# Modulation sums as two-part rows, with four tiles for their weights

## The chip, the cores and the metric

The kernel runs on one core of one Trainium2 chip. The core has TensorE (matmuls; PE in the profile, its weight loads PEld), VectorE (DVE), ScalarE (ACT), GpSimd (POOL) and SyncE (SP), which issues DMAs. TensorE writes to PSUM banks, the other engines and the DMAs work on SBUF tiles. The metric is the device time of one execution in microseconds (us); lower is better. Each engine runs its own list of instructions in a fixed order, and semaphores make one engine wait for another. The order within an engine's list is set when the kernel is built: a planner takes the instructions in the order of the source and lets one that it holds to be ready go ahead, unless it is tied to its place.

## The reference

One layer of a decoder trunk on 1024 tokens of 1024 channels. Six modulation vectors are made from one condition vector; shift and scale enter ahead of each sub-layer, the gates behind it.

```python
cond = jax.nn.silu(c)
mod = cond @ w_ada[l] + b_ada[l]
shift1, scale1, gate1, shift2, scale2, gate2 = jnp.split(mod[:, None, :], 6, axis=-1)
u = x * (1.0 + scale1) + shift1
hq, hf, hi, hg, rq, rk, rv, rg, ga, gb = jnp.split(u @ w_in[l], split_at, axis=-1)
ya = _hgrn2(hq, hf, hi, hg, lower_bounds[l]) @ w_pa[l]
yb = _retention(rq, rk, rv, rg, positions) @ w_pb[l]
y = (jax.nn.sigmoid(ga) * ya + jax.nn.sigmoid(gb) * yb) @ w_o[l]
x = _layer_norm(DEEPNORM_ALPHA * x + (1.0 + gate1) * y, ln1_g[l], ln1_b[l])
u = x * (1.0 + scale2) + shift2
h = jnp.square(jax.nn.relu(u @ w_up[l] + b_up[l]))
y = h @ w_down[l] + b_down[l]
x = _layer_norm(DEEPNORM_ALPHA * x + (1.0 + gate2) * y, ln2_g[l], ln2_b[l])
```

The change concerns `gate1`, `shift2`, `scale2` and `gate2`: four sums of 1024 values, each over 1024 weights.

## The kernel before

All large products run in two-part arithmetic: `split` makes of a number a rounded part `hi` on ScalarE (L172) and the remainder `lo` on VectorE (L173), and `mm3` issues three matmuls, hi with hi, hi with lo and lo with hi (L177 to L179), in a number format in which TensorE takes 512 columns in one step. Products of the input and output projections go by a scheme of seven products for eight; `seven` (from L434) does this for groups of 256 output columns. One group is seven products of twelve matmuls, in PSUM banks named psd, psa and psc. Its operands are pieces `raw` of the weights, loaded by SyncE (L315, four buffers), added or subtracted by VectorE (L223) and split. The sums of products are made by VectorE (L443, which must have read a bank before TensorE writes the next product into it) and handed to `use`: for gates a sigmoid on ScalarE (L705), a multiplication on VectorE (L707) and a store by GpSimd (L708). `seven` yields three times a group.

The stretch of the kept groups (`build`, L1781 to L1786) runs 24 of these: four of hg, four of ga, then rq, rg, rk, rg for each of four heads. Beside those that are not rq or rk, it advances the generator `ada_rest`, once at each of the group's three yields and once more at the third, so four steps a group.

`ada_rest` (L1174) makes the modulation sums. There are 16 of them, four sections by four groups of 256 columns, each in four parts `q`. One step loads a weight tile `adw` of 256 rows two parts ahead (L1184, two buffers) and adds its two halves, times the condition, to an accumulator of 128 partitions by 256 columns on VectorE (`ada_step`, L575 and L576; the first of a step is tied to its place on VectorE). The sum over the 128 partitions is then left, and two steps later `ada_end` (L1207) makes it:

- for gate1 and gate2 `ada_row` (L1213): a full-precision matmul with a column of ones as the stationary operand gives one row of 256 (L1216), a bias row is loaded (L1218) and added together with 1 (L1219), and GpSimd stores the row in DRAM, in `g_d` (L1220).
- for scale2 and shift2 `ada_cols` (L578): two matmuls with the accumulator as the stationary operand and the ones as a moving column give two columns (L582), and one VectorE operation adds the bias and writes them to the tile `mod` (L584). `ada_cols` serves the start of the kernel, too, for shift1 and scale1.

`out_proj` (L1381) is the second place. It loads the row of gate1 to all partitions (L1385), prepares the last merge (`first`, with `merge_gate`, L1235 to L1239), and runs eight token blocks, each two halves of 24 matmuls. After the first block `coefs` (L1395) makes of scale2 and shift2, taken from `mod`, the tile `u2AB` (L1398 to L1400), and the rows RA and RB. One block later `out_second` turns the normalized block on TensorE (L1463) and applies `u2AB` on ScalarE (L1468).

In the printed code below the diff's functions stand with the line numbers of the profile.

Of the kernel before, what the change touches and what calls it, by code (L numbers as in the profile page):

```python
# [10 lines left out]
F32 = mybir.dt.float32  # L11
F32R = mybir.dt.float32r
# [3 lines left out]
ALU = mybir.AluOpType  # L16
# [87 lines left out]
def drain(g):  # L104
    for _ in g:
        pass
# [20 lines left out]
class Trunk:  # L127
# [390 lines left out]
    def consts(self):  # L518
        nc, i = self.nc, self.i
        cp = self.cp  # L520
        self.cst = cp.tile([P, N_CONST], F32, name="cst")
        crow = self.st.tile([8, P], F32, name="crow")
        nc.scalar.dma_start(crow, i["c"].rearrange("o (k p) -> (o k) p", p=P))
        nc.sync.dma_start(self.cst, i["k_const"])
        rows = self.st.tile([P, P], F32, name="rows")
        nc.gpsimd.memset(rows, 0.0)
        for r0, ap, n in ((B_ADA, i["b_ada"], 48), (B_LB, i["lb_logits"], 8), (B_G1, i["ln1_g"], 8),
                          (B_B1, i["ln1_b"], 8), (B_UP, i["b_up"], 32)):
            nc.scalar.dma_start(rows[r0:r0 + n, :], ap.rearrange("o (k p) -> (o k) p", p=P))
        self.mask8 = cp.tile([P, N_MASK8], U8, name="mask8")  # L530
        self.ident = self.cst[:, K_ID:K_ID + P]
        small = self.small = cp.tile([P, 72], F32, name="small")
        self.ones = small[:, 0:1]
        nc.vector.memset(self.ones, 1.0)
        self.mhalf = self.small[:, 8:16]
        nc.vector.memset(self.mhalf, -0.5)
        c = self.small[:, 16:24]
        pc = self.ps("c", (P, 8))
        nc.tensor.transpose(pc, crow, self.ident[:8, :8])
        nc.vector.tensor_copy(c, pc)  # L540
        sg = self.small[:, 24:32]
        nc.scalar.activation(sg, c, AF.Sigmoid)
        self.cond = self.small[:, 32:40]
        nc.vector.tensor_tensor(self.cond, c, sg, op=ALU.mult)

        self.mod = cp.tile([P, 48], F32, name="mod")
        self.cols = cp.tile([P, P], F32, name="cols")
        self.rows = rows

# [624 lines left out]
    def ada_rest(self):  # L1174

        ap = self.aw
        parts = [(s, g, q) for s, g in ADA_ORDER for q in range(4)]
        loaded = {}

        def load(n):  # L1180
            s, g, q = parts[n]
            c0 = s * D + 256 * g
            t = loaded[n] = ap.tile([P, 2, 256], F32, tag="adw", bufs=2, name=self.uid("adw"))
            self.nc.sync.dma_start(t, self.i["w_ada"][256 * q:256 * q + 256, c0:c0 + 256].rearrange("(k p) c -> p k c", p=P))  # L1184

        load(0)
        load(1)
        yield
        ends = None
        for n, (s, g, q) in enumerate(parts):  # L1190
            if q == 0:
                acc = ap.tile([P, 256], F32, tag="adacc", bufs=2, name=self.uid("acc"))
            w = loaded.pop(n)
            for j in (0, 1):
                r = self.ada_step(acc, w[:, j], 2 * q + j, q + j == 0)
                if j == 0:
                    self.tc.keep_in_program_order(r)
            if n + 2 < len(parts):
                load(n + 2)
            if q == 1 and ends is not None:  # L1200
                ends()
            if q == 3:
                ends = lambda acc=acc, s=s, g=g: self.ada_end(acc, s, g)
            yield
        ends()

    def ada_end(self, acc, sec, g):  # L1207
        if sec in (S_SHIFT2, S_SCALE2):
            self.ada_cols(acc, sec, 2 * g, 2, 1.0 if sec == S_SCALE2 else 0.0, self.ps("b", (P, 2)))
        else:  # L1210
            self.ada_row(acc, sec, g)

    def ada_row(self, acc, sec, g):  # L1213
        nc = self.nc
        pr = self.ps("b", (1, 256))
        nc.tensor.matmul(pr, self.ones, acc, start=True, stop=True)  # L1216
        br = self.aw.tile([1, 256], F32, tag="brow", bufs=1, name=self.uid("brow"))
        nc.sync.dma_start(br, self.i["b_ada"][0:1, sec * D + 256 * g:sec * D + 256 * g + 256])  # L1218
        nc.vector.scalar_tensor_tensor(br, pr, 1.0, br, op0=ALU.add, op1=ALU.add)  # L1219
        nc.gpsimd.dma_start(self.g_d[sec][0:1, 256 * g:256 * g + 256], br)  # L1220


# [158 lines left out]
    def out_proj(self, first):  # L1381
        nc, V, i = self.nc, self.nc.vector, self.i
        op = self.op
        s2, h2 = self.mod[:, S_SCALE2 * 8:S_SCALE2 * 8 + 8], self.mod[:, S_SHIFT2 * 8:S_SHIFT2 * 8 + 8]
        g1 = self.row(op, self.g_d[S_GATE1], "g1")  # L1385
        xts = []

        def x_rows(t):
            xts.append(self.wr.tile([P, D], F32, tag="raw", bufs=4, name=self.uid("xt")))
            nc.sync.dma_start(xts[t], i["x"][t * P:(t + 1) * P, :])  # L1390

        x_rows(0)
        x_rows(1)

        def coefs():  # L1395
            AB = op.tile([P, 16], F32, name="u2AB")
            A, B = AB[:, 0:8], AB[:, 8:16]
            V.tensor_tensor(A, self.cols[:, B_G1:B_G1 + 8], s2, op=ALU.mult)  # L1398
            V.tensor_tensor(B, self.cols[:, B_B1:B_B1 + 8], s2, op=ALU.mult)
            V.tensor_tensor(B, B, h2, op=ALU.add)  # L1400
            RA = self.row(op, i["ln1_g"], "RA")
            RB = self.row(op, i["ln1_b"], "RB")
            V.tensor_scalar(RA, RA, ALPHA, None, op0=ALU.mult)
            for j in range(2):
                js = slice(j * 512, j * 512 + 512)
                tt = op.tile([P, D], F32, tag="zp", bufs=1, name=self.uid("rb"))
                t0, t1 = tt[:, :512], tt[:, 512:]
                nc.sync.dma_start(t0, self.g_d[S_GATE2][:, js].to_broadcast([P, 512]))
                nc.sync.dma_start(t1, i["b_down"][:, js].to_broadcast([P, 512]))
                V.tensor_tensor(t0, t0, t1, op=ALU.mult)  # L1410
                V.scalar_tensor_tensor(RB[:, js], RB[:, js], ALPHA, t0, op0=ALU.mult, op1=ALU.add)
            return A, B, RA, RB

        def y_parts(t):
            yh = self.wp.tile([P, 8, P], F32R, tag="wh", bufs=3, name=self.uid("yh"))
            yl = self.wp.tile([P, 8, P], F32R, tag="wl", bufs=3, name=self.uid("yl"))
            for q in (0, 1):
                ks = slice(4 * q, 4 * q + 4)
                self.split(yh[:, ks], yl[:, ks], self.y[q, t // 4][:, :, t % 4 * P:t % 4 * P + P])
            return yh, yl  # L1420

        ys = [y_parts(0)]
        first()
        ys.append(y_parts(1))
        for t in range(8):
            yh, yl = ys.pop(0)
            if t < 6:
                ys.append(y_parts(t + 2))
            xt = xts[t]
            z = op.tile([P, D], F32, tag="z", bufs=2, name=self.uid("z"))  # L1430
            stat = op.tile([P, 32], F32, tag="stat", bufs=2, name=self.uid("stat"))
            for ch in (0, 1):
                cs = slice(ch * 512, ch * 512 + 512)
                po = self.ps("d" if t else "c")
                for k in range(KT):
                    self.mm3(po, yh[:, k], yl[:, k], self.wo[k][0][:, 0, cs], self.wo[k][1][:, 0, cs], k == 0, k == KT - 1)
                V.tensor_tensor(z[:, cs], po, g1[:, cs], op=ALU.mult)
                V.scalar_tensor_tensor(z[:, cs], xt[:, cs], ALPHA, z[:, cs], op0=ALU.mult, op1=ALU.add)
                V.bn_stats(stat[:, 6 * ch:6 * ch + 6], z[:, cs])
            mv, rs = self.norm_stats(stat)  # L1440
            nm = stat[:, 24:25]
            V.scalar_tensor_tensor(nm, mv[:, 0:1], -1.0, rs, op0=ALU.mult, op1=ALU.mult)
            nc.scalar.activation(z, z, AF.Identity, scale=rs, bias=nm)
            if t < 6:
                x_rows(t + 2)
            self.tick()
            if t == 0:
                cf = coefs()
            self.later(1, lambda t=t, z=z: self.out_second(t, z, *cf))
            if t == 6:  # L1450
                self._split_to(self.w_next + 1)
# [220 lines left out]
def build(ctx, tc, ins, out):  # L1672
# [15 lines left out]
             for j in range(FT // 2)]  # L1688
    k.b12_d = k.dp.tile([P, 2048], F32, name="b12_d")
    k.z2_d = [k.dp.tile([P, D], F32, name=f"z2_d{t}") for t in range(8)]  # L1690
    k.g_d = {s: k.dp.tile([1, D], F32, name=f"g_d{s}") for s in (S_GATE1, S_GATE2)}
    w_in = ins["w_in"]


# [207 lines left out]
```

## Time and profile before

| | |
|---|---|
| median of 3 runs | 2258.92 us (2257.53 to 2260.2) |
| profiled execution | 2258.29 us |
| its span, first to last instruction | 2256.5 us |
| granted TensorE clock over the span | 0.997 |
| stretch of the kept groups and the modulation sums | 312 to 797 us |
| output projection, first blocks | 1533 to 1557 us |

A row of the timeline reads: start in us from the start of the span, duration, engine, line, operation, out<-in by the program's tiles with buffer numbers left out, shapes, count; in brackets the idle time just before it and what ended it. A row of the waits reads: who waited, for whom, microseconds in total, times, the longest. A row of the groups reads: line, engine, operation, tiles, shapes, count, busy microseconds, mean nanoseconds of one, and idle time ahead of them. A matmul's record is longer than the distance to the next one's start, since matmuls overlap. "psb" is the bank that the modulation sums use.

### The profile page before, as it was taken

To read this page: it belongs to the slowest core of one execution; us is meant where nothing else is said; L and a number is where in the kernel's file an instruction comes from. 1 tells how busy PE (TensorE), PEld (TensorE's weight loads), DVE (VectorE), ACT (ScalarE), POOL (GpSimd) and SP (SyncE) were. 2 spreads that over 40 slices of the span, in tenths; PEclk is the share of its full clock that TensorE was granted. 3 is DMA by queue.
4 is the path that set the end of the run, shared out by engine and by line. 5 is a ranking of instruction groups with operands and counts; after the bars stand their busy time and mean duration, and the time that the engine had idled before them with its cause. 6 is when DMAs were issued, how large, how long until landed. Compare 5 with 4: busy or idle time off the path is not lost. (4 is left out here: it accounts for less than half of the span.)

```text
span 2256.5 us, 29106 instructions
## 1 busy us (share of the span) xinstructions
PE 2215.7 (98%) x10214; PEld 1822.1 (81%) x10214; DVE 1660.4 (74%) x3024; ACT 967.3 (43%) x1625; POOL 282.1 (13%) x444
## 2 busy tenths in 40 slices
PE   6999999999999999999999999999999999999997
PEld 4888887888888888888877777888878888888886
DVE  7757777667878678889765556977796665577669
ACT  3533334433333333332354434443575555553441
POOL 0110111111111101010112221112112112100001
PEclk9999999999999999999999999999999999999999
DMA  9554644544343522113176667655344444787653
GB/s 309 183 167 161 208 136 164 169 135 140 135 141 117 172 89 75 57 66 104 60 254 201 209 204 258 211 163 179 112 150 156 152 154 151 265 289 247 215 164 131
DMA packets 229075, 375.33 MB, mean 166 GB/s; under 512 B 17096, under 2 KB 127424, under 8 KB 228672
## 3 DMA queue, kind: packets, MB, share of 16 engines
q1 hardware_dynamic: 200176, 279.66, 38.4%
q0 software_dynamic: 28432, 93.35, 11.2%
q8 instruction: 80, 1.31, 0.2%
q14 instruction: 67, 0.55, 0.1%
q10 hardware_dynamic: 320, 0.45, 0.1%
HBM read 275.87 MB, written 97.53 MB: 165 GB/s over the span
## 5 line engine op out<-in xcount | busy, mean ns | idle before, releaser
L177 PE MATMUL psd<-U,bh 128*128 128x512 f32 x616 | 241.9, 393 | 1.8 <-DVE e L443 1.8
L178 PE MATMUL psd<-U,bh 128*128 128x512 f32 x616 | 239.8, 389 | 0.0
L179 PE MATMUL psd<-U,bl 128*128 128x512 f32 x616 | 239.8, 389 | 0.0
L172 ACT ACTIVATE bh<-s 128x512 fp32r<-128x512 f32 x204 | 128.6, 631 | 239.7 <-PE psd L178 78.9
L178 PE MATMUL psd<-U,wh 128*128 128x512 f32 x504 | 199.6, 396 | 3.6 <-DVE U L173 3.3
L177 PE MATMUL psd<-U,wh 128*128 128x512 f32 x504 | 202.4, 405 | 0.4 <-ACT U L172 0.4
L179 PE MATMUL psd<-U,wl 128*128 128x512 f32 x504 | 201.8, 400 | 0.0
L172 ACT ACTIVATE bh<-raw 128x512 fp32r<-128x512 f32 x153 | 97.1, 638 | 206.1 <-PE psd L178 100.4
L173 DVE TENSOR_TENSOR bl<-raw,bh 128x512 fp32r<-128x512 f32 x153 | 104.5, 689 | 105.8 <-ACT bh L172 92.9
L173 DVE TENSOR_TENSOR bl<-s,bh 128x512 fp32r<-128x512 f32 x204 | 139.5, 685 | 49.4 <-ACT bh L172 49.3
L177 PEld LDWEIGHTS psd<-U,bh 128*128 128x128 f32 x616 | 115.6, 188 | 31.0 <-issue 3.5
L172 ACT ACTIVATE U<-hr 128x512 fp32r<-128x512 f32 x112 | 70.5, 630 | 151.0 <-issue 56.7
L179 PEld LDWEIGHTS psd<-U,bl 128*128 128x128 f32 x616 | 115.7, 188 | 24.2
L178 PEld LDWEIGHTS psd<-U,bh 128*128 128x128 f32 x616 | 115.7, 188 | 23.5
L172 ACT ACTIVATE wh<-raw 128x512 fp32r<-128x512 f32 (+1 forms) x78 | 52.7, 695 | 173.8 <-PE psd L178 136.2
L177 PE MATMUL psa<-U,bh 128*128 128x512 f32 x312 | 121.4, 389 | 0.0
L178 PE MATMUL psa<-U,bh 128*128 128x512 f32 x312 | 121.4, 389 | 0.0
L179 PE MATMUL psa<-U,bl 128*128 128x512 f32 x312 | 121.4, 389 | 0.0
L178 PEld LDWEIGHTS psd<-U,wh 128*128 128x128 f32 x504 | 95.5, 190 | 25.3 <-DVE U L173 7.3
L177 PEld LDWEIGHTS psd<-U,wh 128*128 128x128 f32 x504 | 95.1, 190 | 19.1 <-ACT U L172 2.3
L179 PEld LDWEIGHTS psd<-U,wl 128*128 128x128 f32 x504 | 95.3, 189 | 18.7
L173 DVE TENSOR_TENSOR U<-hr,U 128x512 fp32r<-128x512 f32 x112 | 76.7, 685 | 44.7 <-ACT U L172 44.5
(446 smaller groups left out, 5630.7 us busy)
## 6 DMA issues: line engine op xcount, KB each, us to landing
raw<-in_w_in SPq DMA_DIRECT2D x126, 512.0 KB
raw<-in_w_down SPq DMA_DIRECT2D x48, 512.0 KB
raw<-in_w_pb SPq DMA_DIRECT2D x36, 512.0 KB
adw<-in_w_ada SPq DMA_DIRECT2D x64, 256.0 KB
raw<-in_w_up SPq DMA_DIRECT2D x32, 512.0 KB
adw<-in_w_ada SPq DMA_DIRECT2D x16, 512.0 KB
rv_d<-e POOLq DMA_DIRECT2D x32, 256.0 KB, 3.8
rg_d<-e POOLq DMA_DIRECT2D x32, 256.0 KB, 2.4
```

The source lines that it names most:

```text
L172: pin(self.nc.scalar.activation(hi, src, AF.Copy))
L173: pin(self.nc.vector.tensor_tensor(lo, src, hi.bitcast(F32), op=ALU.subtract))
L177: r = mm(out, wh, uh, start=start, stop=False, skip_group_check=more)
L178: mm(out, wh, ul, start=False, stop=False, skip_group_check=more)
L179: return r, mm(out, wl, uh, start=False, stop=stop, skip_group_check=more)
```

## The change

- All four sections become rows. `ada_end` is gone, and `ada_rest` no longer calls `ada_cols`. `mod` shrinks to the 16 columns of shift1 and scale1.
- A row is made in two parts: the accumulator is split into `hi` (ScalarE) and `lo` (VectorE, tied to its place), and two matmuls with a column of ones add both up in one bank. The number format is that of the large products.
- `ada_row` is a generator: bias load and `hi` in one step, `lo` in the next, the matmuls in the next, the bias addition (tied to its place) and the store in the last. With each part of the next sum it advances by one.
- The weight tiles `adw` have four buffers instead of two, the bias row two instead of one; loads are issued two parts ahead, as before.
- At the output projection two small DMAs bring the rows of scale2 and shift2 as 8 x 128 each into a tile of 16 partitions, and `coefs` turns it on TensorE into 16 columns in PSUM, from which `u2AB` is made.
- The scratch for the descriptors of GpSimd's DMAs is set to 4096 bytes a partition; before, nothing was set.

```diff
-        self.mod = cp.tile([P, 48], F32, name="mod")
+        self.mod = cp.tile([P, 16], F32, name="mod")
...
-            t = loaded[n] = ap.tile([P, 2, 256], F32, tag="adw", bufs=2, name=self.uid("adw"))
+            t = loaded[n] = ap.tile([P, 2, 256], F32, tag="adw", bufs=4, name=self.uid("adw"))
...
+        ones = ap.tile([P, 1], F32R, name="ones_r")
+        self.nc.scalar.activation(ones, self.ones, AF.Copy)
         load(0)
         load(1)
         yield
-        ends = None
+
+        ends = iter(())
...
             if n + 2 < len(parts):
                 load(n + 2)
-            if q == 1 and ends is not None:
-                ends()
+            next(ends, None)
             if q == 3:
-                ends = lambda acc=acc, s=s, g=g: self.ada_end(acc, s, g)
+                ends = self.ada_row(acc, s, g, ones)
             yield
-        ends()
-
-    def ada_end(self, acc, sec, g):
-        if sec in (S_SHIFT2, S_SCALE2):
-            self.ada_cols(acc, sec, 2 * g, 2, 1.0 if sec == S_SCALE2 else 0.0, self.ps("b", (P, 2)))
-        else:
-            self.ada_row(acc, sec, g)
-
-    def ada_row(self, acc, sec, g):
-        nc = self.nc
+        drain(ends)
+
+    def ada_row(self, acc, sec, g, ones):
+
+        nc, ap = self.nc, self.aw
+        pin = self.tc.keep_in_program_order
+        hi, lo = (ap.tile([P, 256], F32R, tag="ad" + e, bufs=1, name=self.uid("ad" + e)) for e in "hl")
+        br = ap.tile([1, 256], F32, tag="brow", bufs=2, name=self.uid("brow"))
+        nc.sync.dma_start(br, self.i["b_ada"][0:1, sec * D + 256 * g:sec * D + 256 * g + 256])
+        nc.scalar.activation(hi, acc, AF.Copy)
+        yield
+        pin(nc.vector.tensor_tensor(lo, acc, hi.bitcast(F32), op=ALU.subtract))
+        yield
         pr = self.ps("b", (1, 256))
-        nc.tensor.matmul(pr, self.ones, acc, start=True, stop=True)
-        br = self.aw.tile([1, 256], F32, tag="brow", bufs=1, name=self.uid("brow"))
-        nc.sync.dma_start(br, self.i["b_ada"][0:1, sec * D + 256 * g:sec * D + 256 * g + 256])
-        nc.vector.scalar_tensor_tensor(br, pr, 1.0, br, op0=ALU.add, op1=ALU.add)
+        nc.tensor.matmul(pr, ones, hi, start=True, stop=False)
+        nc.tensor.matmul(pr, ones, lo, start=False, stop=True)
+        yield
+        plus = 0.0 if sec == S_SHIFT2 else 1.0
+        pin(nc.vector.scalar_tensor_tensor(br, pr, plus, br, op0=ALU.add, op1=ALU.add))
         nc.gpsimd.dma_start(self.g_d[sec][0:1, 256 * g:256 * g + 256], br)
...
     def out_proj(self, first):
...
-        s2, h2 = self.mod[:, S_SCALE2 * 8:S_SCALE2 * 8 + 8], self.mod[:, S_SHIFT2 * 8:S_SHIFT2 * 8 + 8]
         g1 = self.row(op, self.g_d[S_GATE1], "g1")
+        mrow = op.tile([16, P], F32, name="mrow")
+        for j, sec in enumerate((S_SCALE2, S_SHIFT2)):
+            nc.sync.dma_start(mrow[8 * j:8 * j + 8], self.g_d[sec].rearrange("o (k p) -> (o k) p", p=P))
...
         def coefs():
             AB = op.tile([P, 16], F32, name="u2AB")
+            m2 = self.ps("a", (P, 16))
+            nc.tensor.transpose(m2, mrow, self.ident[:16, :16])
+            s2, h2 = m2[:, 0:8], m2[:, 8:16]
...
-    k.g_d = {s: k.dp.tile([1, D], F32, name=f"g_d{s}") for s in (S_GATE1, S_GATE2)}
+    k.g_d = {s: k.dp.tile([1, D], F32, name=f"g_d{s}") for s in (S_GATE1, S_SHIFT2, S_SCALE2, S_GATE2)}
...
-    nc = bacc.Bacc("TRN2", target_bir_lowering=False, num_devices=1)
+    nc = bacc.Bacc("TRN2", target_bir_lowering=False, num_devices=1, dynamic_dma_scratch_size=4096)
```

## The prediction

> **What bounds the kernel.** I read the page's busy shares first, then a table of busy time by stretch, then TensorE's waits in the longest stretch that the change touches, and then the timeline around each of its instructions.
>
> ```profile
> PE 2215.7 (98%) x10214; PEld 1822.1 (81%) x10214; DVE 1660.4 (74%) x3024; ACT 967.3 (43%) x1625; POOL 282.1 (13%) x444
> ...
> 312.00:797.00 485.00, 483.19 (x2133) 394.41 (x2132) 359.85 (x625) 186.21 (x316) 60.20 (x112) 1.00 0.45 148
> ...
> PE psd L177 <- DVE e L443: 1.8, 3, 0.7
> ```
>
> TensorE is busy for 98% of the span. The second row gives a stretch, its length, each engine's busy time (TensorE, its weight loads, VectorE, ScalarE, GpSimd), the granted clock and the DMA share. In the stretch from 312 to 797 us, in which the modulation sums are made beside the kept gates, it is busy for 483.19 of 485 us at a granted clock of 1.00. The last row is all that it waited for there: three waits, 1.8 us together. So whatever only unburdens VectorE, ScalarE or a queue can bring these 1.8 us and the restarts behind them, and no more. Otherwise the span moves by what TensorE itself is given to do, and the main term of the sum is what a modulation sum costs on TensorE.
>
> **Removed from TensorE.** Its busy time doesn't show that cost, because matmuls overlap; the distance from start to start does.
>
> ```profile
> 350.61 0.39 PE L177 MATMUL psd<-U,bh 128*128 128x512 f32 x1
> ...
> 353.11 0.39 PE L179 MATMUL psd<-U,bl 128*128 128x512 f32 x1
> 353.42 0.59 PE L1216 MATMUL psb<-acc,small 128*1 128x256 f32 x2
> 353.95 0.50 PE L177 MATMUL psd<-U,bh 128*128 128x512 f32 x1
> 354.29 0.40 PE L178 MATMUL psd<-U,bh 128*128 128x512 f32 x1
> ...
> 550.48 0.39 PE L179 MATMUL psd<-U,bl 128*128 128x512 f32 x1
> 550.71 0.50 PE L582 MATMUL psb<-small,acc 128*128 128x1 f32 x4
> 551.07 0.49 PE L177 MATMUL psd<-U,bh 128*128 128x512 f32 x1
> 551.39 0.40 PE L178 MATMUL psd<-U,bh 128*128 128x512 f32 x1
> ...
> L1219 DVE SCALAR_TENSOR_TENSOR brow<-psb,brow 1x256 f32<-1x256 f32 x8 | 3.2, 405 | 0.0
> ...
> L584 DVE SCALAR_TENSOR_TENSOR mod<-psb,cols 128x2 f32<-128x2 f32 x8 | 1.3, 158 | 1.4 <-PE psb L582 1.3
> ```
>
> From 350.61 to 353.11 lie eleven steps between matmuls of 512 columns, so one step is 0.227 us. Around the row sum, two such steps (353.11 to 354.29) take 1.18 instead of 0.454 us: a full-precision row costs 0.73 us. Around the column sum they take 0.91 (550.48 to 551.39): it costs 0.46 us. The last two rows count them, eight of each: 8 x 0.73 + 8 x 0.46 = **9.5 us removed**.
>
> **Added to TensorE: sixteen rows in two parts.** Each is two matmuls of 256 columns with one stationary column, in the number format of the large matmuls around them. No row shows that form. From below, a 512-column step halved is 0.114, so a row costs 0.23; from above, it costs the 0.73 of the full-precision row. I take 0.30: the format is that of the matmuls before and after, which follow each other without a gap, and 0.07 is left for what a change of shape may cost. So 16 x 0.30 = **4.8 us added** (3.6 to 11.7).
>
> [...]
>
> **What the parts cost the other engines.** Each row needs a copy `hi` on ScalarE and a subtraction `lo` on VectorE, both 128x256.
>
> ```profile
> L173 DVE TENSOR_TENSOR bl<-raw,bh 128x512 fp32r<-128x512 f32 x70 | 47.6, 689 | 38.8 <-ACT bh L172 26.2 <-PE psb L1216 12.4
> ...
> L173 DVE TENSOR_TENSOR U<-U,U 128x1024 fp32r<-128x1024 f32 x2 | 2.4, 1224 | 1.1 <-ACT U L172 1.1
> ...
> L172 ACT ACTIVATE bh<-raw 128x512 fp32r<-128x512 f32 x70 | 45.2, 646 | 112.5 <-PE psd L178 64.1 <-issue 27.1 <-DVE e L727 14.3
> ```
>
> 512 elements more cost VectorE 535 ns, so 256 elements take about 689 - 268 = 421 ns (estimate); half of ScalarE's 646 and some fixed part give about 0.4. Sixteen subtractions are 6.7 us. Eight additions of 405 ns replace eight of 158: 2.0 more. VectorE goes from 359.85 to some 369 of 485 us, ScalarE from 186 to 193. Both have free time in the stretch, so by themselves these cost nothing; without that cover they would be 8.7 us. Eight more bias loads on SyncE and eight more row stores on GpSimd are hidden by those queues' waiting.
>
> **Four tiles for the weights.** Loads are still issued two parts ahead, but into a buffer whose last reader finished long ago.
>
> ```profile
> SPq L1184 <- DVE acc L576: 345.7, 61, 18.3
> ...
> 498.40 0.37 SPq L1184 DMA_DIRECT2D adw<-in_w_ada  x1
> 499.04 1.08 SPq L315 DMA_DIRECT2D raw<-in_w_in  x2
> ...
> 504.97 0.69 DVE L223 TENSOR_TENSOR s<-raw,raw 128x512 f32<-128x512 f32 x1 [3.58 <-DMA raw<-in_w_in]
> ...
> 508.24 0.69 DVE L443 TENSOR_TENSOR e<-psd,e 128x512 f32<-128x512 f32 x1
> ...
> 508.99 0.50 PE L177 MATMUL psd<-U,bh 128*128 128x512 f32 x1 [0.67 <-DVE e L443]
> 509.32 0.40 PE L178 MATMUL psd<-U,bh 128*128 128x512 f32 x1
> ```
>
> SyncE's 345.7 us of waiting for the accumulation should go, but TensorE felt them only in the three waits. The one at 508.99 shows the way: a 256 KB weight load starts 0.64 us ahead of two 512 KB projection pieces; they land at 504.97, VectorE starts its burst late, and L443 frees the bank late. One MB in 5.9 us is 0.17 MB per us, so the load ahead takes about 1.5 us. Issued earlier, it is out of the way. Against this, the bias addition now sits in that part, before the split that frees the pieces: 0.4 later. A wait also costs a slow restart (0.33 for a step of 0.227). All three waits gone would be 1.8 + 3 x 0.1 = 2.1 us. I take **-1.3** (-2.1 to +1.3, three waits longer by the 0.4).
>
> **At the output projection.** Two small DMAs, one transpose and three VectorE operations that now wait for it.
>
> ```profile
> 1538.83 0.38 SPq L1369 DMA_DIRECT2D g<-g_d  x1
> 1539.32 0.37 SPq L1235 DMA_DIRECT2D gbr<-gb_d  x1
> ...
> 1541.20 0.15 DVE L1398 TENSOR_TENSOR u2AB<-cols,mod 128x8 f32<-128x8 f32 x1
> ...
> 1541.47 1.30 DVE L1400 TENSOR_TENSOR u2AB<-u2AB,mod 128x8 f32<-128x8 f32 x1
> ...
> 1544.39 0.69 DVE L1238 TENSOR_TENSOR U<-psb,gbr 128x512 f32<-128x512 f32 x1 [1.62 <-DMA gbr<-gb_d]
> ...
> 1556.26 1.09 PE L1463 MATMUL psa<-cst,z 128*128 128x128 f32 x8 [0.94 <-ACT z L1443]
> ```
>
> The DMAs go behind g on SyncE's queue and push the merge's gate load (1539.32) back by about 0.7 us. VectorE waits for that load until 1544.39, and the chain from there to the z of the first token block is what TensorE waits for at 1556.26. The three coefficient operations lay in VectorE's idle time from 1541.20 on; behind the transpose, which in the source follows the first block's 48 matmuls, they fall into the same chain: 3 x 0.15. So that wait grows by about **1.1 us** (0, if the order leaves both out of the chain, to 2.3, if one of the three takes 1.30 as the last did). The transpose waits for the small DMAs, and the second block's matmuls stand behind it; the first block's 10.9 us (48 x 0.227) should cover their landing. The transpose itself is **0.25** (from 0.14, an eighth of the 1.09 above, to 0.73).
>
> **At the stretch's end** the last row, now in more steps, holds its buffers longer.
>
> ```profile
> L1220 POOL DMA_DIRECT2D g_d<-brow x8: 505/505/523, 356.6 to 514.9; - x8
> ...
> DMA to landing us min/median/max: 1.9/2.8/3.3
> ...
> 791.43 3.44 SPq L315 DMA_DIRECT2D raw<-in_w_in  x4
> ...
> 800.00:804.00 4.00, 4.00 (x19) 3.34 (x18) 0.00 (x0) 1.20 (x2) 0.00 (x0) 1.00 1.04 365
> ...
> 804.02 0.63 ACT L172 ACTIVATE wh<-raw 128x512 fp32r<-128x512 f32 x1 [2.82 <-PE psd L178]
> ```
>
> Copy, subtraction, matmuls, addition (0.4 each, 0.3 for the matmuls), the issue (0.5) and the landing (2.8) of a store are 4.8 us. SyncE's queue, with four weight loads, may wait for that release; its transfers, done by 804 now (DMA share 1.04 up to there), would then be done by 809. The split at 804.02 could come that much later. It prepares a weight tile two ahead of the one in use, so TensorE need not notice, and I take nothing (up to 4.8, if VectorE's work behind that split is late for TensorE).
>
> **The sum.** -9.5 + 4.8 - 1.3 + 1.1 + 0.25 = -4.65 us. The profiled execution took 2258.29 (span 2256.5 and 1.8 around it), so it would take 2253.6; from the median shown, 2258.92, **2254.3 us**.
>
> **Rivals.**
>
> (1) *TensorE waits for `lo`.* Before, the accumulated tile was long done when its matmul came up. Now the matmul needs a VectorE result of the same step.
>
> ```profile
> 354.62 0.68 DVE L707 TENSOR_TENSOR e<-e,psd 128x512 f32<-128x512 f32 x1
> ...
> 355.95 1.50 DVE L576 SCALAR_TENSOR_TENSOR acc<-adw,small,acc 128x256 f32<-128x256 f32 x3
> ...
> DVE s L223 <- DMA raw<-in_w_in: 44.3, 22, 3.6
> ```
>
> The subtraction would come behind the first of the three at 355.95 and end near 356.85, 3.4 us after the place of today's row. The order on TensorE is fixed when the kernel is built; if it puts the row too early, every matmul behind it waits. The three waits above show that such an order can err by 0.6 us when VectorE is late, and VectorE waited 22 times for pieces. With 0.3 us for each of 16 rows the gain is gone: -4.65 + 4.8, or 2259.1 (chance 0.19). With 0.6 it is -4.65 + 9.6: **2263.9, slower**; slower by over 0.2% from 0.57 us a row on (chance 0.13). For it: nothing separates `lo` and its matmul in the source's steps. Against it: in 21 of 24 groups TensorE met no late VectorE.
>
> (2) *The two-part row is as dear as the full-precision one*: 16 x 0.73 = 11.7, so -4.65 + 6.9: 2261.2 (0.06).
>
> (3) *All falls well*: rows of 0.23, no waits, nothing at the output projection: -9.5 + 3.6 - 2.1 + 0.15 = -7.85: 2251.1 (0.10).
>
> (4) *GpSimd's stores wait for room in a smaller descriptor scratch.*
>
> ```profile
> q0 software_dynamic: 28432, 93.35, 11.2%
> ...
> or_d<-ot POOLq DMA_DIRECT2D x32, 256.0 KB, 4.8
> ```
>
> 28432 packets are 1777 on each of 16 engines. The slowest frequent store lands after 4.8 us; if one store ahead of the norm's power on GpSimd had to wait so long, the end moves by up to 4.8: 2259.1 (0.03). [...]
>
> (5) *The four tiles do nothing*, since loads are still two ahead: without the -1.3, 2255.6. It lies within the forecast's own range, 2251.8 to 2256.8 (0.46). Some other shift of the built order: 0.03.
>
> **Range and chances.** A measurement of this kernel can tell about 0.2%, 4.5 us, from no change: below 2254.4 is faster, above 2263.4 slower. The forecast sits on the first bound, and I give 0.32 of its 0.46 to faster, since its large terms are measured and only 0.30 a row is chosen. With (3), 0.10, and 0.03 of the rest: faster 0.45. Same: 0.14 + 0.18 + 0.06 + 0.02 = 0.40. Slower: 0.13 + 0.02 = 0.15. The range reaches from 2249 to 2263.5: below it is only the lower end of (3), above it most of the slower case, together some 0.15.
>
> **What would show it.** Right: 16 rows at which two steps take about 0.75 us in place of 1.18 and 0.91; no wait of TensorE in the stretch; SyncE's wait for the accumulation near zero; TensorE's wait at the first block's transposes near 2 us. Wrong: a TensorE wait named after `lo` at the rows (rival 1), a row's two steps near 1.2 (rival 2), or a transpose of the sums that waits for its small DMAs.

## The result, and the profile after

The changed kernel takes 2268.36 us (median of 6 runs, 2266.34 to 2274.94), the kernel before 2258.31 us (6 runs, 2256.36 to 2260.2). The ratio is 1.0054 [1.0044, 1.0064]: **0.5% slower**, 14 us above the forecast and 5 us above its range. The profiled execution took 2268.21 us, 9.9 more than the one of before.

The first fence has rows of the page of the changed kernel, the second its busy time by stretch (columns as in the prediction), the third the later of these stretches in the kernel before, the fourth the changed kernel's waits of TensorE and VectorE from 312 to 807 us.

```profile
PE 2217.7 (98%) x10199; PEld 1822.4 (80%) x10199; DVE 1664.3 (73%) x3040; ACT 973.8 (43%) x1642; POOL 287.5 (13%) x452
...
L177 PE MATMUL psd<-U,bh 128*128 128x512 f32 x616 | 242.4, 393 | 11.3 <-DVE e L443 11.3
```

```profile
312.00:480.00 168.00, 168.00 (x747) 137.69 (x747) 118.77 (x214) 74.11 (x128) 20.70 (x39) 1.00 0.52 167
480.00:797.00 317.00, 305.72 (x1331) 247.91 (x1330) 242.08 (x421) 113.40 (x197) 41.40 (x77) 0.99 0.41 132
```

```profile
480.00:797.00 317.00, 315.19 (x1400) 259.52 (x1400) 246.22 (x422) 114.28 (x194) 37.09 (x69) 1.00 0.42 140
```

```profile
PE psd L177 <- DVE e L443: 11.3, 7, 2.2
...
DVE s L223 <- DMA raw<-in_w_in: 54.4, 22, 5.1
```

TensorE's busy share is still 98%, and up to 480 us it waits for nothing. The loss is in the second part of the stretch: 305.72 us busy of 317, where the kernel before is busy for 315.19. The 1.8 us of waits for L443 have become 11.3, in seven waits in place of three, and VectorE's wait for the projection pieces has grown from 44.3 to 54.4 us.

Where the time went is seen when the same instruction is found in two traces. The table gives by how many us a ScalarE instruction starts later (+) or earlier (-) than in the profiled execution of the kernel before. Each kernel is described below.

| at (us) | changed | e2 | e6 | e7 | e11 |
|---|---|---|---|---|---|
| 310, stretch begins | -2.1 | -1.6 | -1.0 | -1.3 | -1.2 |
| 500 | -5.1 | -4.4 | -1.0 | -1.3 | -4.2 |
| 800, stretch over | +7.1 | -6.5 | +8.2 | -0.8 | -5.0 |
| last one | +9.9 | -7.2 | +7.8 | -0.6 | -4.8 |

The first line differs by a microsecond or two between executions whatever the kernel. From 310 to 500 the changed kernel gains 3.0 us; from 500 to 800 it loses 12.2. The stretch as a whole costs 9.2 of the 9.9; what follows scatters by a few us each way.

One of the seven stalls, of the changed kernel, by engine in the timeline (GpSimd, SyncE, VectorE, TensorE):

```profile
614.12 0.54 POOL L708 DMA_DIRECT2D rg_d<-e  x1 [2.26 <-DVE e L707]
614.83 0.51 POOL L1226 DMA_DIRECT2D g_d<-brow  x1 [0.17 <-issue]
```

```profile
614.25 0.37 SPq L1184 DMA_DIRECT2D adw<-in_w_ada  x1
615.20 1.30 SPq L315 DMA_DIRECT2D raw<-in_w_in  x2
```

```profile
614.14 0.41 DVE L1225 SCALAR_TENSOR_TENSOR brow<-psb,brow 1x256 f32<-1x256 f32 x1
614.47 1.27 DVE L173 TENSOR_TENSOR bl<-raw,bh 128x512 fp32r<-128x512 f32 x2
...
621.96 0.69 DVE L223 TENSOR_TENSOR s<-raw,raw 128x512 f32<-128x512 f32 x1 [5.13 <-DMA raw<-in_w_in]
...
625.24 0.68 DVE L443 TENSOR_TENSOR e<-psd,e 128x512 f32<-128x512 f32 x1
```

```profile
623.38 0.39 PE L179 MATMUL psc<-U,bl 128*128 128x512 f32 x1
625.98 0.80 PE L177 MATMUL psd<-U,bh 128*128 128x512 f32 x1 [2.21 <-DVE e L443]
626.57 0.63 PE L178 MATMUL psd<-U,bh 128*128 128x512 f32 x1
627.00 0.63 PE L179 MATMUL psd<-U,bl 128*128 128x512 f32 x1
...
630.12 0.40 PE L179 MATMUL psd<-U,bl 128*128 128x512 f32 x1
630.36 0.28 PE L1221 MATMUL psb<-adh,ones_r 128*1 128x256 f32 x1
630.48 0.39 PE L177 MATMUL psd<-U,bh 128*128 128x512 f32 x1
```

The row's end (bias addition L1225, store L1226) now falls right ahead of two 512 KB pieces of the next projection weight. The store stands on GpSimd's queue behind the 256 KB store of the kept gate (`rg_d`), 0.37 us before the pieces are issued. VectorE uses them at 621.96, 6.8 us after their issue; in the kernel before it was 4.7 in the groups without a stall and 5.9 in the three with one. VectorE's burst starts late, L443, which stands behind that first L223 in VectorE's fixed order, frees the bank late, and TensorE waits 2.2 us. In the kernel before the row's end came two steps earlier, in part 1 of the next sum and not in part 3; no pair of pieces follows there.

The last three lines show a new row: 630.12 to 630.48 is 0.36 for a step of 0.227, so its first matmul costs 0.13. All sixteen rows, taken so, cost 4.2 us.

### The profile page after: what moved, and what is told of

The parts are those of the page before. It is cut to its first block, busy times and chain, and to the rows that moved or that the text cites. A ratio compares the mean times of both kernels' runs of the same rounds, so it can differ in the third digit from the quotient of the medians.

```text
span 2266.4 us, 29143 instructions
## 1 busy us (share of the span) xinstructions
PE 2217.7 (98%) x10199; PEld 1822.4 (80%) x10199; DVE 1664.3 (73%) x3040; ACT 973.8 (43%) x1642; POOL 287.5 (13%) x452
## 3 DMA queue, kind: packets, MB, share of 16 engines
q0 software_dynamic: 28688, 93.36, 11.1%
## 5 line engine op out<-in xcount | busy, mean ns | idle before, releaser
L177 PE MATMUL psd<-U,bh 128*128 128x512 f32 x616 | 242.4, 393 | 11.3 <-DVE e L443 11.3
```

The lines of the kernel that those rows point to most:

```text
L177: r = mm(out, wh, uh, start=start, stop=False, skip_group_check=more)
```

## The experiments

Three theories at first. **A**: the row's store delays the pieces behind it. **B**: the bias addition, ahead of the pieces' splits on VectorE, delays their issue and use. **C**: the four tiles change the order of the loads. Behind e8 two more share A between them: **S**, the store's packets of 64 bytes are what hurts, and **Q**, any store at that place in GpSimd's queue. The ratio is to the kernel before, run beside each group of experiments; its medians there were 2257.62 to 2258.87 us, so a difference between runs of different groups is good to about 1 us. "Waits" are TensorE's for L443 from 312 to 807 us.

| | us (range, runs) | ratio to before | waits: us, times, longest |
|---|---|---|---|
| e1 | 2259.92 (2258.21 to 2262.79, 10) | 1.0008 [0.9999, 1.0018] | 6.5, 7, 1.3 |
| e2 | 2252.84 (2251.0 to 2257.11, 10) | 0.998 [0.9971, 0.999] | 1.5, 2, 0.8 |
| e3 | 2270.13 (2266.37 to 2272.36, 4) | 1.0056 [1.0041, 1.0071] | 14.2, 7, 3.1 |
| e4 | 2256.45 (2253.78 to 2261.02, 10) | 0.9996 [0.9987, 1.0006] | 3.0, 3, 1.2 |
| e5 | 2267.32 (2265.11 to 2270.63, 4) | 1.0044 [1.0027, 1.0061] | 11.1, 7, 2.1 |
| e6 | 2269.24 (2266.03 to 2271.89, 4) | 1.0047 [1.0032, 1.0062] | 10.2, 6, 2.0 |
| e7 | 2257.33 (2255.87 to 2260.17, 10) | 0.9998 [0.9989, 1.0007] | 2.1, 3, 1.0 |
| e8 | 2259.3 (2255.69 to 2259.8, 10) | 1.0002 [0.9992, 1.0011] | 3.4, 3, 1.2 |
| e9 | 2268.23 (2266.68 to 2271.1, 4) | 1.0044 [1.0027, 1.0061] | 11.4, 6, 2.2 |
| e10 | 2257.44 (2256.21 to 2260.68, 10) | 1.0002 [0.9992, 1.0011] | 3.2, 3, 1.3 |
| e11 | 2254.12 (2251.39 to 2258.14, 10) | 0.9978 [0.9969, 0.9987] | 1.8, 4, 0.6 |
| e12 | 2253.64 (2251.38 to 2259.41, 10) | 0.9981 [0.9971, 0.999] | 1.1, 1, 1.1 |

**e1, the store one step later.** In the changed kernel, with room for two rows on their way and three bias rows:

```diff
         pin(nc.vector.scalar_tensor_tensor(br, pr, plus, br, op0=ALU.add, op1=ALU.add))
-        nc.gpsimd.dma_start(self.g_d[sec][0:1, 256 * g:256 * g + 256], br)
+        yield
+        pin(nc.gpsimd.dma_start(self.g_d[sec][0:1, 256 * g:256 * g + 256], br))
```

> The changed kernel with one thing moved: the row's store to DRAM is issued one step later (behind the second gate store of its group instead of the first), while the bias addition stays where it is on VectorE; a third bias buffer carries the row over. Theory A (the store's sixteen 64-byte packets, sent 0.37 us ahead of two 512 KB weight pieces, delay these by about 1.2 us, and TensorE waits): pieces land 4.7 to 5.9 us after issue instead of 5.9 to 7.1, TensorE's waits for L443 in the stretch fall from 11.3 to about 3 us, the stretches of half clock behind waits of 2.2 us vanish, 2257 us. Theory B (VectorE's bias addition ahead of the pieces' splits, and TensorE arriving earlier, make the waits): nothing changes, 2268 us. Theory C (the order of the four weight tiles' loads): nothing changes, 2268 us.

8.4 us come back, so the store's place is most of the loss. Seven waits stay, shorter. In them the pieces are used 5.0 to 6.2 us after their issue.

**e2, bias addition and store two steps later**, and so in part 1 again, of the sum after the next:

```diff
         nc.tensor.matmul(pr, ones, lo, start=False, stop=True)
         yield
+        yield
+        yield
         plus = 0.0 if sec == S_SHIFT2 else 1.0
```

> The changed kernel with bias addition and store both moved two steps later, to the group's third yield, where the row's end stood before. Theories A and B: the waits go back to those of before or fewer, 2254 to 2256 us (the two-part rows' saving of about 5.3 us is then left). B alone against A: the gain over the run with only the store moved is then 3 us or more; with A alone it is 1 to 2 us, the 0.3 us by which the pieces are issued sooner. Theory C: 2266 to 2268 us.

15.5 us faster than the changed kernel, and apart from the same room for more rows as in e1 the only edit is the place of the row's end. It is 0.2% faster than the kernel before. Five of its seven uses of a pair come 4.6 to 4.75 us after the issue. In the other two (6.0 and 6.1) the packets show a 16 KB instruction fetch beside the pieces; these two are its waits.

**e3, two weight tiles** in the changed kernel, and **e4, four tiles and the smaller descriptor scratch** in the kernel before:

```diff
-            t = loaded[n] = ap.tile([P, 2, 256], F32, tag="adw", bufs=4, name=self.uid("adw"))
+            t = loaded[n] = ap.tile([P, 2, 256], F32, tag="adw", bufs=2, name=self.uid("adw"))
```

```diff
-            t = loaded[n] = ap.tile([P, 2, 256], F32, tag="adw", bufs=2, name=self.uid("adw"))
+            t = loaded[n] = ap.tile([P, 2, 256], F32, tag="adw", bufs=4, name=self.uid("adw"))
...
-    nc = bacc.Bacc("TRN2", target_bir_lowering=False, num_devices=1)
+    nc = bacc.Bacc("TRN2", target_bir_lowering=False, num_devices=1, dynamic_dma_scratch_size=4096)
```

> The changed kernel with two weight tiles instead of four. Theory A and theory B: as the changed kernel, 2266 to 2270 us, waits of 10 to 12 us. Theory C (four tiles put a weight load 0.96 instead of 0.64 us ahead of the pieces and another between them): 2258 to 2261 us, waits of 2 to 4 us.

> The kernel before with four weight tiles and the smaller descriptor scratch alone, no rows changed. Theory A and theory B: as before, 2257 to 2260 us, TensorE's waits in the stretch 1 to 3 us. Theory C: 2265 us or more. If the smaller scratch slows GpSimd's stores, it shows here as well, as stores that land later than 2.4 us.

C falls: with two tiles the changed kernel is as slow, and four tiles and the small scratch cost the kernel before nothing. The -1.3 us of the forecast lies within the interval of e4, and so does nothing at all.

**e5, the store alone put back.** e2, with room for one row and one bias row more, and in it

```diff
         pin(nc.vector.scalar_tensor_tensor(br, pr, plus, br, op0=ALU.add, op1=ALU.add))
-        nc.gpsimd.dma_start(self.g_d[sec][0:1, 256 * g:256 * g + 256], br)
+        yield
+        yield
+        pin(nc.gpsimd.dma_start(self.g_d[sec][0:1, 256 * g:256 * g + 256], br))
```

**e6 and e7, more stores in the kernel before**: sixteen at the bad place (e6) and fifteen, of the sum before, at the good one (e7; `prev` is that sum's accumulator). They go to a scratch `g_x` in DRAM that is declared for them, and nobody reads what they store:

```diff
             if q == 3:
+                self.tc.keep_in_program_order(self.nc.gpsimd.dma_start(self.g_x[0:1, 64 * (n - q):64 * (n - q) + 256], acc[0:1, :]))
                 ends = lambda acc=acc, s=s, g=g: self.ada_end(acc, s, g)
```

```diff
             if q == 1 and ends is not None:
                 ends()
+                self.tc.keep_in_program_order(self.nc.gpsimd.dma_start(self.g_x[0:1, 64 * (n - q):64 * (n - q) + 256], prev[0:1, :]))
```

**e8, a VectorE operation more in the kernel before:**

```diff
             if q == 3:
+                self.tc.keep_in_program_order(self.nc.vector.scalar_tensor_tensor(acc, acc, 1.0, acc, op0=ALU.mult, op1=ALU.max))
                 ends = lambda acc=acc, s=s, g=g: self.ada_end(acc, s, g)
```

> The kernel of e2 (2252.84 us) with only the store of the row moved two further steps on, so that it stands again where a pair of 512 KB pieces is about to be issued; the bias addition stays at its late, harmless place, and VectorE's and TensorE's orders are those of e2. Theory A (the store's 64-byte packets delay the pieces): its 8.4 us come back, 2261, with TensorE's waits for L443 near 7 us. Theory B (the bias addition in front of the splits is what counts, the store only goes with it): 2253, waits near 1.5 us. If the cost of the store needs both, something between.

> The kernel before, whose row ends stay where they are, with one more store of 1 KB in each of the sixteen groups, of the first row of the accumulated tile to a scratch in DRAM, on GpSimd right after the group's last accumulation, where the changed kernel has its row's store. VectorE, TensorE and ScalarE run their old order. Theory A: some 8 us slower than before, 2266, with TensorE waiting for L443 in most of the later groups. Theory B: as before, 2258.

> The same sixteen extra stores in the kernel before, two steps later, beside the row ends of the kernel before, where no pair of pieces follows. Theory A and theory B: as before, 2258 (to 2260), so that a slower e6 is due to the place and not to sixteen more transfers. If it is as slow as e6, the place doesn't matter.

> The kernel before with one more VectorE operation in each group at that place, right after the group's last accumulation and ahead of the pieces' splits: the accumulated tile times 1.0, maximum with itself (128x256, some 0.45 us, leaves the values as they are). No store is added. Theory B: the pieces' buffers come free and their splits end later, TensorE waits for L443: 5 to 7 us slower, 2263 to 2265. Theory A: VectorE has free time, 2258 to 2260.

These settle A. The store alone, put back into e2, costs 14.5 us (2267.32 - 2252.84); e6 loses 10.9 us to before and e7 nothing, by the same store at another place, and in both the other engines keep the order of the kernel before (in e6 but for one instruction of VectorE and one of SyncE, near 800 us). Six of seven pairs in e6 meet the store 0.23 us ahead of them and stall; at the seventh it is issued 2.65 us behind the first piece (and the kept gate's store 2.12 us behind it), the pieces are used after 4.3 us, and TensorE doesn't wait. A large store ahead of the small one in the queue doesn't do the harm by itself: in six of e7's later groups the small store stands 0.53 us behind a gate's store, too, and there the next piece, a single one, follows 1.87 us behind it. e8 shows no loss, but tells less of B than meant: in the later groups its operation came between the splits that free the two pieces, so that only the second was issued later, by 0.33 us.

The pair of e6 that is looked at next, with the queues of GpSimd and SyncE and the first use:

```profile
538.49 0.51 POOL L1203 DMA_DIRECT2D g_x<-acc  x1
```

```profile
538.73 1.08 SPq L315 DMA_DIRECT2D raw<-in_w_in  x2
```

```profile
545.86 0.69 DVE L223 TENSOR_TENSOR s<-raw,raw 128x512 f32<-128x512 f32 x1 [4.78 <-DMA raw<-in_w_in]
```

What the store does to the transfers is seen in a table by stretch: one pair of pieces in e7 and the same pair in e6, in 1 us from 1 us behind the first piece's issue. The last two columns are the DMA engines' mean busy share and GB/s.

```profile
538.29:539.29 1.00, 1.00 (x6) 0.84 (x5) 0.34 (x1) 1.00 (x2) 0.00 (x0) 1.00 0.88 300
539.29:540.29 1.00, 1.00 (x6) 0.81 (x5) 0.35 (x1) 0.11 (x1) 0.00 (x0) 1.00 1.03 378
540.29:541.29 1.00, 1.00 (x6) 0.84 (x5) 0.00 (x0) 0.28 (x1) 0.00 (x0) 1.00 1.10 380
541.29:542.29 1.00, 1.00 (x6) 0.84 (x5) 0.22 (x1) 0.35 (x1) 0.00 (x0) 1.00 1.02 359
542.29:543.29 1.00, 1.00 (x6) 0.81 (x6) 1.00 (x3) 0.00 (x0) 0.00 (x0) 1.00 0.27 91
```

```profile
539.72:540.72 1.00, 1.00 (x6) 0.84 (x5) 0.33 (x1) 1.00 (x2) 0.00 (x0) 1.00 0.92 315
540.72:541.72 1.00, 1.00 (x6) 0.82 (x5) 0.36 (x1) 0.12 (x1) 0.00 (x0) 1.00 0.76 239
541.72:542.72 1.00, 1.00 (x6) 0.83 (x5) 0.00 (x0) 0.28 (x1) 0.00 (x0) 1.00 0.86 201
542.72:543.72 1.00, 1.00 (x6) 0.84 (x5) 0.00 (x0) 0.36 (x1) 0.00 (x0) 1.00 0.80 250
543.72:544.72 1.00, 1.00 (x6) 0.81 (x6) 0.00 (x0) 0.00 (x0) 0.00 (x0) 1.00 0.91 315
544.72:545.72 1.00, 1.00 (x6) 0.84 (x5) 0.00 (x0) 0.00 (x0) 0.00 (x0) 1.00 0.35 121
545.72:546.72 1.00, 1.00 (x7) 0.81 (x5) 0.86 (x2) 0.00 (x0) 0.00 (x0) 1.00 0.19 66
```

Without the store all sixteen engines are busy and move 360 to 380 GB/s until the pieces are there. With it the transfers run at 200 to 250 GB/s in the same microseconds, with engines idle although a megabyte is due, and end in a tail in which a few engines catch up. The drop begins with the store: its sixteen packets start from 2.0 to 2.9 us behind the first piece's issue, which is the second row of e6. A store of 1 KB costs the pieces some 2.4 us (used after 7.14 in e6, 4.78 in e7).

**e9 and e10, which property of the store.** e6 with sixteen rows of 1 KB, and e6 with the store on SyncE's queue:

```diff
+                self.tc.keep_in_program_order(self.nc.gpsimd.dma_start(self.g_x[4 * (n - q):4 * (n - q) + 16, :], acc[0:16, :]))
```

```diff
+                self.tc.keep_in_program_order(self.nc.sync.dma_start(self.g_x[0:1, 64 * (n - q):64 * (n - q) + 256], acc[0:1, :]))
```

> e6 again (the kernel before with a store on GpSimd at the bad place, 2269.24 us), but of sixteen rows of 1 KB in place of one: sixteen packets of 1024 bytes, where e6 has sixteen of 64. Theory S (the size: packets of 64 bytes hold up the engines that carry the pieces): 2258 to 2260, though 16 KB move instead of 1. Theory Q (any store at this place, queued on GpSimd behind the 256 KB store of the kept gate, has the pieces wait): 2266 to 2270.

> e6 again, with its 1 KB store issued by SyncE, between the two pieces, in place of GpSimd, and so not behind the 256 KB store of the kept gate. The second piece is issued some 0.4 us later for it. Theory S: as slow as e6, 2266 to 2270, if SyncE's store is cut into packets of 64 bytes too. Theory Q: 2258 to 2261.

S falls: sixteen packets of 1024 bytes are as bad as sixteen of 64 (2268.23 and 2269.24 us). Q fits both runs, but the queue isn't shown alone. From SyncE, where the packets show the row as one of 1024 bytes, the store costs nothing, though it stands between the two pieces and puts the second off to 0.97 us or more behind the first. So e10 changes three things at once: the queue, one packet in place of sixteen, and the place behind the first piece. No run separates them. These are the two queues of e10 around the same pair:

```profile
538.35 0.54 POOL L708 DMA_DIRECT2D rg_d<-e  x1 [2.32 <-DVE e L707]
```

```profile
538.48 0.37 SPq L1184 DMA_DIRECT2D adw<-in_w_ada  x1
539.11 0.37 SPq L315 DMA_DIRECT2D raw<-in_w_in  x1
539.53 0.50 SPq L1203 DMA_DIRECT2D g_x<-acc  x1
540.08 0.37 SPq L315 DMA_DIRECT2D raw<-in_w_in  x1
```

**e11 and e12, the store from SyncE** in the changed kernel and in e2:

```diff
-        nc.gpsimd.dma_start(self.g_d[sec][0:1, 256 * g:256 * g + 256], br)
+        nc.sync.dma_start(self.g_d[sec][0:1, 256 * g:256 * g + 256], br)
```

> The changed kernel with one word altered: the row's store is issued by SyncE in place of GpSimd, at the same step, and so not behind the kept gate's 256 KB store. The bias addition stays at its early place. VectorE's built order moves the first two L223 of the later groups behind one more operation, since the pieces now stand behind the store. Theory Q with a bias addition that costs nothing by itself: 2252 to 2254, as e2. Theory Q with the bias addition's early place worth the 7 us that lie between e1 and e2: 2258 to 2261. If GpSimd's queue is not the point: 2268.

> e2 (bias addition and store both at the late place, 2252.84 us) with the store issued by SyncE. VectorE's and TensorE's orders are those of e2. Theory Q: at the late place GpSimd's store did no harm, so 2252 to 2254, the same; if its packets still cost something there, 2250 to 2251.

One word turns the changed kernel into one of 2254.12 us, 14.2 us faster and 0.2% faster than the kernel before. But the built order of VectorE changes with it, so that this isn't the worth of the store's queue alone. e12, whose VectorE order is that of e2, adds nothing to e2. The three fast versions (e2, e11, e12) can't be told apart.

B is left half open. In e11 the bias addition keeps its early place, and the pieces are still used late (5.3 to 6.4 us after their issue), yet TensorE's waits are 1.8 us: in each of the seven groups the order built for VectorE has an L443 and a split ahead of the first L223 that stand behind it in the changed kernel, so that late pieces hold up less. In e1, with VectorE in the order of the changed kernel, the pieces come as late (5.0 to 6.2), and the early bias addition goes with 6.5 us of waits and 7.1 us more than e2. So an early bias addition can cost, next to a tight order; on top of the harmful store it added at most 1.0 us (2268.36 against e5, whose ranges overlap).

## Why the prediction was wrong

**The rows: right.** Removed 9.5, added 4.8 foretold; added 4.2 measured, 0.26 a row (0.24 where both matmuls stand together). The forecast's lower bound, half of a 512-column step for each of a row's two matmuls, was 0.23 a row: the trace is within 0.03 of it. With 9.5 less 4.2, 5.3 us, this term is about the gain that e2, e11 and e12 show (4.8 to 5.4 us).

**The row stores: the step that failed.** "Eight more bias loads on SyncE and eight more row stores on GpSimd are hidden by those queues' waiting." The step counted the new stores and not the new place of all sixteen: behind the kept gate's store and just ahead of two pieces. GpSimd is busy for only 62.1 of the 485 us from 312 to 797 (20.70 and 41.40); what isn't hidden is the transfer, which meets the loads that set TensorE's pace. Foretold 0, measured 14.5 (e5 against e2). The trace of the changed kernel accounts for it: 11.3 - 1.8 = 9.5 of waits, 0.16 for each of four more waits (a matmul is drawn 0.39 long and followed after 0.227), and 3.7 more for restarts (5 of 0.15 and 2 of 1.7, against 3 of 0.15): 13.8. Less the 5.3 saved at the rows, that is 8.5; the stretch lost 9.2.

**Four tiles, -1.3: wrong in its reason, small in its size.** "Issued earlier, it is out of the way" did not come true. SyncE's waits ahead of the weight loads are still there, as this table of the changed kernel's waits from 312 to 807 us shows: four buffers fill, and the loads wait for VectorE again (by these rows for the bias addition, the accumulation or the subtraction `lo`), and one still goes out right ahead of the pieces (0.95 us, 614.25 to 615.20).

```profile
SPq L1184 <- DVE brow L1225: 144.6, 12, 19.0
...
SPq L1184 <- DVE acc L576: 96.4, 23, 7.8
...
SPq L1184 <- DVE adl L1218: 70.9, 14, 6.9
```

Nor was the load ahead the cause of the three waits of the kernel before: there it is issued 0.64 us ahead of all seven pairs, also of the four that are used after 4.7 us. What sets the three apart in the packets is an instruction fetch (last section).

The upper bound of this term, "three waits longer by the 0.4", named the bias addition and not the store beside it, and took the number of waits for fixed. But the three groups that waited had used their pieces 1.1 us later than the four that didn't, and had waited 0.6 us each (1.8 / 3), so the four had only about 0.5 us to spare.

**Output projection, +1.1: not seen.** The changed kernel's TensorE doesn't wait at the first transposes at all, and the three operations start at 1555.31 and end by 1556.91 beside other work. The 0.94 us wait that the term was added to isn't there in every execution: of the other runs with the old code, e6, e7, e8 and e10 don't have it, and e4 and e9 have 0.6 and 0.4 us. The transpose's 0.25 can't be seen either.

```profile
1555.31 0.15 DVE L1409 TENSOR_TENSOR u2AB<-cols,psa 128x8 f32<-128x8 f32 x1
...
1556.04 0.16 DVE L1410 TENSOR_TENSOR u2AB<-cols,psa 128x8 f32<-128x8 f32 x1
...
1556.76 0.15 DVE L1411 TENSOR_TENSOR u2AB<-u2AB,psa 128x8 f32<-128x8 f32 x1
```

**End of the stretch, 0: right.** The lag is 7.1 us at 800 and 7.3 at 1120.

**The rivals.** (1) had the slower side with a chance of 0.13 but not the cause: no wait of TensorE is named after `lo`, and the rows run at full pace. (2) falls with the 0.26. (4), the smaller scratch, falls with e4. (5), four tiles that do nothing, is what e3 and e4 show, and with the rows it is close to what e11 reached: 2255.6 against 2254.12. The sum was nearly that of the kernel without its harmful store, in part by luck: its -1.3, +1.1 and 0.25 came to nothing and nearly cancel. What was missing was a rival for a small transfer in a bad place, so the range ended at 2263.5.

## What to carry to other kernels

When a step is moved, look up for each of its DMAs what stands ahead of it in its queue and which loads are issued behind it, and price the delay of those loads, not the bytes of the transfer. A small store on GpSimd's queue just ahead of loads that an engine is waiting for is moved by a step or two, or to SyncE, before anything else is tuned (here 11.9 us, e6 against e7, and 11.8, e6 against e10). Look also at what stands behind the first use of such loads in the waiting engine's fixed order. And a profile's single wait (here the 0.94 us) is no base for a term until a second execution shows it.

## What the runs showed of the hardware

- A 1 KB store on GpSimd's queue behind one of 256 KB had 1 MB of loads on SyncE's queue arrive some 2.4 us later (used after 7.14 us in e6, 4.78 in e7), and left DMA engines idle meanwhile: their mean busy share was 0.76 to 0.91 in e6, where e7 has 1.02 to 1.10. Its packet size didn't matter (2269.24 us in e6, 2268.23 in e9), and a few microseconds of its place did (2257.33 in e7). From SyncE, as one packet in place of sixteen and issued behind the first load, it did no harm (2257.44 in e10); which of these three counts is open. So is what the engines wait for.
- TensorE ran at half clock behind its two longest waits of the changed kernel (2.21 and 2.17 us), and a 2.2 us wait so cost 1.6 us more. The rows are 1 us stretches behind the wait shown above; the third column from the end is the granted clock.

```profile
625.98:627.00 1.02, 1.02 (x3) 0.83 (x4) 1.02 (x3) 1.02 (x2) 0.00 (x0) 0.50 0.52 197
627.00:628.00 1.00, 1.00 (x4) 0.81 (x3) 1.00 (x2) 0.10 (x1) 0.18 (x1) 0.50 0.56 158
628.00:629.00 1.00, 1.00 (x4) 0.81 (x3) 1.00 (x3) 0.00 (x0) 0.36 (x1) 0.50 0.59 207
629.00:630.00 1.00, 1.00 (x5) 0.77 (x5) 0.32 (x1) 0.00 (x0) 0.00 (x0) 0.86 0.58 221
```

  In e5 a wait of 2.09 us was followed by half clock and one of 2.14 was not, so the length of a wait alone doesn't tell. In the traces of the kernel before and of the changed one, the changes of the granted clock lie whole multiples of 3.413 us apart (from 3.413 to 2205.010). The two half-clock stretches above are 3.41 us long each, at 625.86 and 748.74 us, and start 122.88 us apart, 36 times 3.413. In the 3.41 us ahead of each, TensorE idled for 2.10 and 2.17 us; behind every other such interval of the changed kernel between 312 and 807 us, with 1.58 us of idling or less, it ran at full clock. The 2.14 of e5 lay across a boundary of these intervals, 0.63 and 1.50. At 1175 us of the changed kernel, outside the stretch, 1.73 us was followed by half clock. What sets the clock is not shown beyond these cases.
- In the groups of the kernel before and of e2 in which the pieces came late without any store ahead of them (5.8 to 6.1 us against 4.7), a 16 KB instruction fetch lies among the packets, and in none of the others. In e4, e7, e8 and e10 the same three groups as in the kernel before have the fetch and are late (5.7 to 6.6 us). In e12 one of two pairs with a fetch was late (6.4) and the other hardly (4.9). No run here took the fetch away.
